# Row maximum norm of an 8192 x 8192 matrix: the SBUF ring and every load at multiples of 512 bytes, and a new list of 33 tail loads

## The chip, the core and the metric

The kernel runs on one core of a Trainium2 chip. The core's engines work side by side, each through its own queue of instructions, and wait for each other on semaphores. Four matter here: the sixteen DMA engines, which copy between HBM (the chip's main memory) and SBUF (the core's working memory of 128 partitions); SP, the queue that issues nearly all of the copies; DVE, the vector engine, which does all of the arithmetic; and Pool, which ends the program. The metric is the device time of one execution in microseconds (us); lower is better. Times come from repeated executions; the profile is one further execution, in which every instruction and every DMA packet is recorded.

## What is computed

```python
def setup_inputs():
    return {"x": np.random.randn(8192, 8192).astype(np.float32)}

def reference(x):
    return np.linalg.norm(x, ord=np.inf, axis=1)
```

For `axis=1` this norm is the largest absolute value of each row. Every one of the 268,435,456 bytes of `x` is read once, and 8192 floats are written.

## The kernel before

The 8192 rows are shared out over 128 partitions, 64 rows to each. Of these, 48 go through the *bulk* and 16 (`n_tail`, the sum of the list `TAIL` over 8192 columns) through the *tail*.

All loads go into one SBUF tile, `ring` (line 229), which holds three slots of 16384 floats in each partition and 256 floats more (`R`, line 214). It is the first tile of the pool. In the built program it begins at byte 16512 of the partition, which is 128 bytes past a multiple of 512; the 128 bytes ahead of it hold four constants of 32 bytes each. The results are collected in `r_bulk` and `r_tail` (lines 230 and 231), behind the ring.

**Bulk** (lines 242 to 250): 24 loads of two rows to each partition. That is 16384 floats, 65536 contiguous bytes, in each of 128 partitions, 8192 KB a load. Load k goes to slot k mod 3. One DVE instruction, `absmax` (lines 233 to 236), reduces it to two maxima. From load 3 on, SP's issue waits until DVE has read what stood in the slot.

**Tail** (lines 253 to 300): in each partition the 16 remaining rows are one run of 131072 contiguous floats, cut into loads whose widths are given by `TAIL`, 31 of them, from 13312 columns down to 576. They are numbered here 24 to 54, after the bulk's 0 to 23. A load can end in the middle of a row, so each load falls into *pieces* of one row each (lines 253 to 261). The piece that ends a row is reduced into `r_tail`. Every other piece is reduced to a partial maximum, which DVE writes into one of the floats of the ring that lie just ahead of the load that will end the row (`slot`, lines 266 to 275). The last piece and its partial maxima are then read in one go: a last piece of 576 columns with nine partial maxima is a read of 585. All in all the tail has 44 reductions.

The place of a load in the ring (lines 270 to 272) is the next multiple of `PAD` = 16 floats, 64 bytes, behind the load before and the room for its partial maxima; where it doesn't fit before the end of the ring, it begins again at the front:

```python
at = -(-(here + n_part) // PAD) * PAD
if at + w > R:
    at = -(-n_part // PAD) * PAD
```

As every width is a multiple of 64 floats, every load reads from a multiple of 256 bytes of `x`. In SBUF six tail loads begin at a multiple of 256 bytes: numbers 26, 29, 34, 37, 38 and 39. All others, the bulk's 24 among them, begin 64, 128 or 192 bytes past one.

**Order.** SP issues the loads in order. An issue waits for DVE where the load overwrites what DVE has to read first, or, as eight semaphores (`DMAHW0` to `DMAHW7`) go round, for the landing of the load eight places before. The order within DVE is that of the loads. The store of `r_bulk` goes out on the queue of ScalarE (ACT) after the last reduction of the third-last load (line 297), and that of `r_tail` on SP after the last reduction (line 301).

Four functions then edit the finished program. `start_first_load_early` puts load 0 ahead of the opening barrier; `drop_implied_waits` takes out waits that another wait covers; `open_without_vector` takes DVE out of the opening barrier; `finish_on_pool` lets Pool alone wait for the last store, after it has cleared the other semaphores. It clears them in one instruction where the last store's semaphore is the first of the range, as here (`DMAHW0`), and otherwise in two, one to each side.

Of the kernel before, what the change touches and what calls it, by code (L numbers as in the profile page):

```python
# [12 lines left out]
F32 = mybir.dt.float32  # L13
X = mybir.AxisListType.X

TAIL = [
    10688, 13312, 11840, 10624, 9472, 8448, 7552, 6720,
    6016, 5376, 4800, 4288, 3904, 3456, 3072, 2688,  # L20
    2432, 2176, 1920, 1728, 1536, 1344, 1280, 1152,
    1024, 896, 832, 704, 640, 576, 576,
]


# [173 lines left out]
@with_exitstack  # L199
def kernel(  # L200
    ctx: ExitStack,
    tc: tile.TileContext,
    x: bass.AP,
    out: bass.AP,
    G: int = 4,
    B: int = 2,
    SLOTS: int = 3,
    PAD: int = 16,
):
    nc = tc.nc  # L210
    P = nc.NUM_PARTITIONS
    rows, cols = x.shape
    W = B * cols
    R = SLOTS * W + PAD * 16


    n_tail = sum(TAIL) // cols
    assert sum(TAIL) == n_tail * cols
    n_bulk_rows = rows // P - n_tail
    assert n_bulk_rows % (G * B) == 0  # L220
    A = n_bulk_rows // (G * B)
    split = n_bulk_rows * P
    x_b = x[:split].rearrange("(a p n b) c -> a n p (b c)", p=P, a=A, n=G, b=B)
    out_b = out[:split].rearrange("(a p n b) -> p a (n b)", p=P, a=A, n=G, b=B)
    x_t = x[split:].rearrange("(p t) c -> p (t c)", p=P)
    out_t = out[split:].rearrange("(p t) -> p t", p=P)

    pool = ctx.enter_context(tc.tile_pool(name="sbuf", bufs=1))
    ring = pool.tile([P, R], F32)
    r_bulk = pool.tile([P, A, G * B], F32)  # L230
    r_tail = pool.tile([P, n_tail], F32)

    def absmax(o, i):
        return nc.vector.reduce_max(  # L234
            out=o, in_=i, axis=X, apply_absolute_value=True
        )

    def after(ins, first, kind):
        info = mybir.DependencyInfo(kind, mybir.DependencyReason.SCHED_ONLY)
        tc.add_manual_dep(ins.ins, first.ins.name, info, reason="order")  # L240

    for a in range(A):
        for n in range(G):
            at = (a * G + n) % SLOTS * W
            t = ring[:, at : at + W]
            nc.sync.dma_start(out=t, in_=x_b[a, n])
            absmax(
                r_bulk[:, a, n * B : (n + 1) * B],
                t.rearrange("p (b c) -> p b c", b=B),
            )  # L250


    pieces, at = [], 0
    for j, w in enumerate(TAIL):
        end = at + w
        while at < end:
            r = at // cols
            to = min(end, (r + 1) * cols)
            pieces.append((j, r, to - at))
            at = to  # L260
    of_row = [[k for k, s in enumerate(pieces) if s[1] == r] for r in range(n_tail)]


    here = A * G % SLOTS * W
    start, slot = [], []
    for j, w in enumerate(TAIL):
        first = next(s for s in pieces if s[0] == j)
        ks = of_row[first[1]]
        n_part = len(ks) - 1 if pieces[ks[-1]][0] == j else 0
# [3 lines that stand above are left out]
        start.append(at)  # L273
        slot.append(at - n_part)
        here = at + w

    src = 0
    for j, w in enumerate(TAIL):
        at = start[j]
        nc.sync.dma_start(out=ring[:, at : at + w], in_=x_t[:, src : src + w])  # L280
        src += w
        here = [k for k, s in enumerate(pieces) if s[0] == j]
        offs = [at + sum(pieces[i][2] for i in here[:m]) for m in range(len(here))]
        todo = list(zip(here, offs))
        if slot[j] != at:

            todo = todo[1:] + todo[:1]
        for k, lo in todo:
            _, r, n = pieces[k]
            ks = of_row[r]  # L290
            if k == ks[-1]:
                frm = slot[j] if len(ks) > 1 else lo
                done = absmax(r_tail[:, r : r + 1], ring[:, frm : lo + n])
            else:
                to = slot[pieces[ks[-1]][0]] + ks.index(k)
                done = absmax(ring[:, to : to + 1], ring[:, lo : lo + n])
        if j == len(TAIL) - 3:

            ins = nc.scalar.dma_start(out=out_b, in_=r_bulk[:])
            after(ins, done, mybir.DependencyClass.Sync)  # L300
    nc.sync.dma_start(out=out_t, in_=r_tail[:])
    nc.at_finalize(drop_implied_waits)
    nc.at_finalize(start_first_load_early)
    nc.at_finalize(finish_on_pool)
    nc.at_finalize(open_without_vector)
# [30 lines left out]
```

## Time and profile before

| What | Value |
|---|---|
| median of 3 runs | 627.94 us (627.76 to 628.19) |
| the profiled execution | 627.77 us, of which 625.1 us are its span |
| bytes moved, mean rate over the span | 268.47 MB, 429 GB/s |
| DVE busy | 553.3 us in 68 reductions (24 bulk, 44 tail) |
| one bulk reduction | 17.22 us |
| one load's issue on SP | 0.33 us |
| last reduction | begins at 623.60 us, takes 0.76 us |
| store of `r_tail` | issued at 624.39 us, lands 1.4 us later |

The span runs from the first instruction to the last; the 2.67 us between it and the time lie around it. The page has a line for each engine's busy time, a row of digits for the share of the DMA engines in 40 equal slices, the DMA queues, and the chain of work that ended last. A load's landing is the moment at which the sixteenth and last increment of its semaphore arrives, one from each DMA engine; the trace keeps the times of all increments, and of every DMA packet its start, duration and size.

### The profile page before, as it was taken

The numbers are of one execution on the slowest core, as the hardware profiler recorded it, in microseconds if no ns is written. First come the engines' busy times: TensorE is split into PE (matmuls) and PEld (weight loads), VectorE is DVE, ScalarE is ACT, GpSimd is POOL, SyncE is SP. The second block draws the span as 40 slices with busy tenths as digits, with TensorE's granted clock in tenths as the row PEclk, the third lists the DMA queues.
The fourth block names the chain that finished last, engine by engine and source line by source line (L and its number), as shares of the span: only waits on it lengthen the run. The fifth ranks groups of instructions, "written<-read, shape, count | busy, mean of one in ns | idle before, by whom it ended". The sixth has DMA issues, their size and how long they took to land.

```text
span 625.1 us, 157 instructions
## 1 busy us (share of the span) xinstructions
DVE 553.3 (89%) x68; POOL 0.2 (0%) x4
## 2 busy tenths in 40 slices
DVE  0588988889988889888898888988889999999999
POOL 0000000000000000000000000000000000000000
DMA  9999999999999999999999999999999999999998
GB/s 403 470 403 457 415 453 419 436 436 415 457 403 470 403 470 403 470 403 457 415 449 424 428 445 403 470 403 470 403 423 450 443 411 441 429 430 423 425 424 333
DMA packets 8705, 268.47 MB, mean 429 GB/s; under 512 B 1664, under 2 KB 1664, under 8 KB 3328
## 3 DMA queue, kind: packets, MB, share of 16 engines
q1 hardware_dynamic: 7920, 268.44, 99.6%
q10 hardware_dynamic: 784, 0.02, 0.1%
q14 instruction: 1, 0.01, 0.0%
HBM read 268.44 MB, written 0.03 MB: 429 GB/s over the span
## 4 chain that ended last, share of the span: by engine, by line
DMA 64%; DVE 35%; another core or an unknown queue 0%; SPq 0%; issue 0%
DMA ring<-in_x_dram 64%; DVE r_bulk L234 25%; DVE ring L234 5%; DVE r_tail L234 5%; SPq L280 0%
## 5 line engine op out<-in xcount | busy, mean ns | idle before, releaser
L234 DVE TENSOR_REDUCE r_bulk<-ring 128x2 f32<-128x16384 f32 x24 | 413.3, 17220 | 70.9 <-DMA ring<-in_x_dram 70.9
L234 DVE TENSOR_REDUCE ring<-ring 128x1 f32<-128x3072 f32 (+25 forms) x28 | 88.8, 3204 | 0.1
L234 DVE TENSOR_REDUCE r_tail<-ring 128x1 f32<-128x8192 f32 (+14 forms) x16 | 53.2, 3330 | 0.1
L320 POOL MEMSET const-bfloat16-1.0<- 128x1 bf16 x1 | 0.1, 102 | 0.0
L320 POOL MEMSET const-uint8-127<- 128x1 uint8 x1 | 0.1, 102 | 0.0
L320 POOL MEMSET const-float32-1.0<- 128x1 f32 x1 | 0.1, 99 | 0.0
L320 POOL MEMSET const-float32-0.0<- 128x1 f32 x1 | 0.1, 98 | 0.2 <-issue 0.2
## 6 DMA issues: line engine op xcount, KB each, us to landing
ring<-in_x_dram SPq DMA_DIRECT2D x1, 6656.0 KB, 30.5
ring<-in_x_dram SPq DMA_DIRECT2D x1, 5920.0 KB, 25.1
ring<-in_x_dram SPq DMA_DIRECT2D x1, 5344.0 KB, 34.1
ring<-in_x_dram SPq DMA_DIRECT2D x1, 5312.0 KB, 37.3
ring<-in_x_dram SPq DMA_DIRECT2D x1, 4736.0 KB, 37.6
ring<-in_x_dram SPq DMA_DIRECT2D x1, 4224.0 KB, 33.5
ring<-in_x_dram SPq DMA_DIRECT2D x1, 3776.0 KB, 30.0
ring<-in_x_dram SPq DMA_DIRECT2D x1, 3360.0 KB, 37.6
```

What stands on the lines that cost most here:

```text
L234: return nc.vector.reduce_max(out=o, in_=i, axis=X, apply_absolute_value=True)
L320: nc = _bacc.Bacc("TRN2", target_bir_lowering=False, num_devices=1)
```

## The change

The ring is allocated last instead of first, behind `r_bulk`, `r_tail` and an unused tile `gap`, whose width brings the ring to a multiple of 512 bytes: in the built program it begins at byte 16896, which is 33 times 512. `PAD` goes from 16 to 128 floats, so every load begins at a multiple of 512 bytes in the partition. The slack behind the three slots goes from 256 to 512 floats. The tail's widths are all multiples of 128 columns, so that every load also reads from a multiple of 512 bytes of `x`; there are 33 loads (24 to 56), from 13440 columns down to 512, instead of 31, and 47 reductions instead of 44. The bulk's loads and reductions are the same in number, size and order.

```diff
+HEAD, STEP = 32, 8
+
 TAIL = [
-    10688, 13312, 11840, 10624, 9472, 8448, 7552, 6720,
-    6016, 5376, 4800, 4288, 3904, 3456, 3072, 2688,
-    2432, 2176, 1920, 1728, 1536, 1344, 1280, 1152,
-    1024, 896, 832, 704, 640, 576, 576,
+    13440, 12800, 11520, 10240, 9088, 8192, 7296, 6528,
+    5760, 5248, 4608, 4096, 3712, 3328, 2944, 2688,
+    2304, 2048, 1920, 1664, 1536, 1408, 1280, 1152,
+    1024, 896, 768, 768, 640, 640, 512, 512,
+    512,
 ]
...
-    PAD: int = 16,
+    PAD: int = 128,
...
-    R = SLOTS * W + PAD * 16
+    R = SLOTS * W + PAD * 4
...
-    ring = pool.tile([P, R], F32)
     r_bulk = pool.tile([P, A, G * B], F32)
     r_tail = pool.tile([P, n_tail], F32)
+    used = [HEAD, A * G * B, n_tail]
+    gap = -sum(-(-n // STEP) * STEP for n in used) % PAD
+    pool.tile([P, gap], F32, name="gap")
+    ring = pool.tile([P, R], F32)
```

Two more loads in the round of eight semaphores move the last store's semaphore from `DMAHW0` to `DMAHW2`, which lies inside the range, so Pool clears in two instructions instead of one.

## The prediction

> **What bounds the kernel now.** I read the page's busy lines first, then the chain of work that ended last, then the timelines of DVE and SP in the tail.
>
> ```profile
> DVE 553.3 (89%) x68; POOL 0.2 (0%) x4
> DMA  9999999999999999999999999999999999999998
> DMA 64%; DVE 35%; another core or an unknown queue 0%; SPq 0%; issue 0%
> L234 DVE TENSOR_REDUCE r_bulk<-ring 128x2 f32<-128x16384 f32 x24 | 413.3, 17220 | 70.9 <-DMA ring<-in_x_dram 70.9
> ```
>
> The DMA engines never rest, and in the bulk DVE is the one that waits: 70.9 us, all of it for loads. The chain, in order of time, gives the pace:
>
> ```profile
> 41.22 17.22 DVE r_bulk L234
> ...
> 466.94 17.22 DVE r_bulk L234
> 484.16 8.59 DVE r_tail L234
> ...
> 608.23 0.02 issue
> 608.25 6.30 DVE ring L234 x4
> ...
> 623.60 0.76 DVE r_tail L234
> ```
>
> Each bulk reduction begins as its load lands: load 1 at 41.22, load 23 at 466.94, so a load lands every 425.72 / 22 = 19.351 us. From 466.94 to the end DVE hardly rests: the tail is 157.4 us of reductions that wait for a landing only here and there, at 608.25 last. So the end hangs on two things: when load 23 lands, and how long DVE's tail takes after it, as long as the loads stay ahead.
>
> **What a start off 256 bytes costs.** In the packet records, packets of 47360 and 10752 bytes (loads 26 and 39, at multiples of 256 bytes) last 1749 and 404 ns: 36608 / 1345 = 27.2 bytes per ns. Each engine carries 8 packets of a load, so a bulk load's bytes alone need 8 x 65536 / 27.2 = 19.275 us; it takes 0.076 more. The tail shows the same excess with both kinds of start side by side. In SP's own timeline each of these issues waits for the landing of the load eight before (36 to 40):
>
> ```profile
> 588.94 0.33 SPq L280 DMA_DIRECT2D ring<-in_x_dram  x1
> 593.02 0.33 SPq L280 DMA_DIRECT2D ring<-in_x_dram  x1
> 596.66 0.33 SPq L280 DMA_DIRECT2D ring<-in_x_dram  x1
> 599.85 0.33 SPq L280 DMA_DIRECT2D ring<-in_x_dram  x1
> 602.78 0.33 SPq L280 DMA_DIRECT2D ring<-in_x_dram  x1
> ```
>
> Loads 37, 38 and 39 took 4.08, 3.64 and 3.19 us; their bytes need 4.066, 3.614 and 3.162. Load 40, which begins 64 bytes off, took 2.93 against 2.861. By the semaphore records, finer than the timeline, the six loads at multiples of 256 land 10, 0, 9, 20, 20 and 27 ns over their bytes, and nearly all others 67 to 90 ns, whether 64, 128 or 192 off.
>
> **Bulk, changed.** All 24 loads now begin at a multiple of 512. The excess of 76 ns can fall to 14 (mean of the six) or 24 (median engine of the last of three such in a row). But another limit stands near: packets on one engine start 2414 ns apart at the closest (1058 gaps in the bulk; two are less), even early, when they run ahead of the landings, and the ninth hand-over, with the semaphore write, adds about 7: 8 x 2414 + 7 = 19.319, an excess of 44. The six aligned loads show 44 to 49 in their packets' ends too; they land faster only because the lag between packet and landing shrinks, from 0.49 to 0.39 us. A lag can't shrink for 24 loads, so I take 44. The gain by load 23 is 23 x (19.351 - 19.319) = 0.73; the other bounds give 23 x 0.052 = 1.20 and 23 x 0.062 = 1.43. No row excludes a loss, but none hints at one; the lower bound is 0.
>
> The Trainium skill, "DMA: Bandwidth & Descriptors", section "How a descriptor splits into AXI transactions", says that a descriptor starting off a multiple of 256 bytes costs a transaction more. The rule asks for 256, so it gives the step from 256 to 512 nothing, and by it alone the whole 8 x 256 / 27.2 = 75 ns would go from each load, an estimate of 1.73 us for the bulk; the packets' spacing says less than half.
>
> **Tail on DVE.** Three reductions more. Durations of 749 ns for 576 columns and 8676 for 8192 give 149 ns fixed, of which 82 overlap the instruction before: 3 x 0.067 = +0.20. Columns are the same. A reduction that waits both for a load and for the partial maximum written just before it starts 34 ns after the one before instead of 82 ns ahead of it; three do so now (593.20, 603.11, 623.60), two will: -0.12. What else keeps DVE waiting in the tail are landings: 26, 13, 61, 208, 24, 49, 26, 10 and 61 ns past the usual overlap, 0.48 in all. If the loads lead, this goes: -0.48. Sum -0.39 (lower bound of the gain: waits stay and +0.08 is left).
>
> **Do the loads lead?** Loads 24 to 54 now land in 623.49 - 466.92 = 156.57 us, 2.37 over their bytes; 0.49 of it is one 8192-byte instruction fetch at 606.7 on one DMA engine (a packet of load 43 lasted 855 ns instead of 265), which the trace shows once in the tail. 33 loads at 0.044, with the fetch, make 1.94, so the last lands at 623.49 - 0.73 - 0.43 = 622.33. DVE's last reduction would end at 624.36 - 0.73 - 0.39 = 623.24, and takes 0.70: it begins at 622.54 and needs the landing 0.11 before. Cover 0.10 us, so DVE decides, just; followed load by load through loads 42 to 47, behind the fetch, the lead is as thin, 0.03 to 0.13. Should the fetch come twice, up to 0.4 of it would show.
>
> The same skill page, "Rules for kernel authors", asks for at least 1 MiB per DMA, which speaks against the new list: 15 loads below that instead of 13. By its table (341 GB/s at 1 MB) the 0.5 MB more in such loads would cost an estimated 0.3 us against the bulk's rate. Here loads of 288 KB land 0.70 to 0.73 us apart, over 400 GB/s.
>
> **Costs that I set at nothing.** SP issues two loads more, 0.33 each; the last is released by a landing seven loads ahead, some 6 us, and a queue is never empty meanwhile (the first packet of a fresh issue comes 1 us later). The store of `r_bulk` leaves after the third-last reduction, about 1.3 us before the last store instead of 1.5, and is down (2.0 us) 0.7 before it (1.4). Pool's extra clear lies in the 0.7 us between the closing barrier and the landing of the last store; Pool's dearest rows are 0.18. Without that cover it costs 0.2 at most. What follows the last reduction, and the 2.67 us around the span, stay.
>
> **Sum.** -0.73 - 0.39 = -1.12 on the profiled 627.77: 626.65. The runs' median is 0.17 above that execution, so 626.8 for the median.
>
> **Rivals.**
> 1. *The packets' spacing falls too.* 2414 may be the price of an unaligned start as well. Then 24 to 14 ns are left: -1.20 or -1.43, and -0.39 in the tail: 626.35 to 626.1. For it: landings came at 14. Against it: the 44 in the aligned loads' packet ends. Chance 0.30.
> 2. *The bulk does not speed up*: the excess belongs to 64 KB packets, not to where they start, and the tail gains at most its waits: 627.94 - 0.39 = 627.55. If starts don't matter at all, so that the change doesn't do what it says, 33 x 0.076 + 0.49 = 3.00 against 2.37 puts the last landing at 624.12 and the end 0.5 later, 628.5. Against it: 76 ns in tail loads of every size off the multiple, and never on it. Chance 0.17.
> 3. *The engines fall into step.* With all starts alike in the 512 bytes, packets of sixteen engines could collide in SBUF as they do when load 0 starts: its packets last 2484 on average, 63 ns over the later 2421, 8 x 63 = 0.50 us a load. In all 24 bulk loads that is +12, near 640. It decides once a bulk load loses 0.10 us ((1.26 + 1.12) / 24). Against it: load 26 begins at a multiple of 512 and took 10 ns over its bytes. Chance 0.05.
>
> **How the numbers follow.** What can be told from no change here is about 0.2%, 1.26 us: below 626.68 is faster, above 629.20 slower. The likeliest case, 0.48, is 626.8, between 626.5 and 627.2 with the fetch and the run-to-run spread; a quarter of it, 0.12, falls on the faster side. Rival 1 is faster (0.30), rival 2 within (0.17), rival 3 slower. So faster 0.42, same 0.53, slower 0.05. The range runs from rival 1's end, 626.0, to the middle of rival 2, 628.0.
>
> **What would show it.** Bulk reductions 19.32 us apart, load 23 landing near 466.2; 19.30 and less is rival 1, 19.35 rival 2. No reduction of the tail waiting for a landing but perhaps one behind the fetch; last reduction ending near 623.2. Packets of 65536 bytes still 2414 ns apart, without the 2418 and 2422 of now. I am wrong if packets start closer than 2414, or if DVE's waits persist because loads of the new tail land later than 0.1 us behind this count.

## The result, and the profile after

| | before | changed |
|---|---|---|
| median | 627.90 us (22 runs) | 626.97 us (22 runs) |
| lowest to highest | 627.72 to 628.33 | 626.61 to 627.65 |
| ratio | | 0.9986, 95% interval 0.9979 to 0.9992 |
| the profiled execution, and its span | 627.77, 625.1 | 627.04, 624.4 |
| load 1's and load 23's reductions begin | 41.22, 466.94 | 41.34, 466.82 |
| from there to the end of the last reduction | 157.42 | 156.83 |

The median fell by 0.93 us, 0.14%: a gain whose interval lies clear of zero, and whose middle lies inside the 0.2% of which the forecast spoke. The forecast was 626.8. The lowest run fell by 1.11 us. In these runs the changed kernel scatters more widely than the kernel before (1.04 us from lowest to highest against 0.61); in the later sets of runs that is not always so.

The page of the changed kernel first (its reductions now stand on line 240):

```profile
DVE 552.8 (89%) x71; POOL 0.2 (0%) x4
...
DMA  9999999999999999999999999999999999999998
...
DMA ring<-in_x_dram 58%; DVE r_bulk L240 25%; DVE ring L240 10%; DVE r_tail L240 6%
...
L240 DVE TENSOR_REDUCE r_bulk<-ring 128x2 f32<-128x16384 f32 x24 | 413.3, 17220 | 70.8 <-DMA ring<-in_x_dram 70.8
```

The picture is the old one: DMA engines never at rest, DVE waiting in the bulk. The change is in the chain of work that ended last, in order of time (start, duration, what):

```profile
41.34 17.22 DVE r_bulk L240
...
234.85 17.23 DVE r_bulk L240
...
408.85 17.23 DVE r_bulk L240
...
466.82 17.22 DVE r_bulk L240
484.04 8.59 DVE r_tail L240
...
592.28 0.02 issue
592.30 6.08 DVE ring L240 x2
...
622.95 0.70 DVE r_tail L240
```

Read it in three steps. From load 1 to load 11 (41.34 to 234.85) a load took 19.351 us, no better than before; from load 11 to load 20 (to 408.85) it took 19.333. Load 23 was 0.12 earlier than before. After it DVE's chain breaks for a landing only once, at 592.30, where before DVE waited in some nine places: 0.59 of the 0.71 us that this execution gained up to the last reduction were gained in the tail.

SP's timeline, with issues that wait for the landings of loads 37 to 40, shows the new pace of the tail:

```profile
592.30 0.33 SPq L286 DMA_DIRECT2D ring<-in_x_dram  x1
595.78 0.33 SPq L286 DMA_DIRECT2D ring<-in_x_dram  x1
598.96 0.33 SPq L286 DMA_DIRECT2D ring<-in_x_dram  x1
601.70 0.33 SPq L286 DMA_DIRECT2D ring<-in_x_dram  x1
```

Loads 38, 39 and 40 took 3.48, 3.18 and 2.74 us; their bytes, at 27.2 per ns, need 3.464, 3.162 and 2.711. How far a load lands *over its bytes* is the time from the landing before to its own, less the time of its bytes at that rate. By the semaphore records the tail loads 25 to 35 land 45 ns over their bytes on average, and 38 to 56 land 36 over.

### The profile page after: what moved, and what is told of

Same layout as the page of the kernel before. It is cut to its first block, busy times and chain, and to the rows that moved or that the text cites. A ratio compares the mean times of both kernels' runs of the same rounds, so it can differ in the third digit from the quotient of the medians.

```text
span 624.4 us, 161 instructions
## 1 busy us (share of the span) xinstructions
DVE 552.8 (89%) x71; POOL 0.2 (0%) x4
## 4 chain that ended last, share of the span: by engine, by line
DMA 58%; DVE 41%; another core or an unknown queue 0%; issue 0%
DMA ring<-in_x_dram 58%; DVE r_bulk L240 25%; DVE ring L240 10%; DVE r_tail L240 6%
## 5 line engine op out<-in xcount | busy, mean ns | idle before, releaser
L240 DVE TENSOR_REDUCE ring<-ring 128x1 f32<-128x512 f32 (+20 forms) x31 | 91.6, 2997 | 0.0
L240 DVE TENSOR_REDUCE r_tail<-ring 128x1 f32<-128x8192 f32 (+12 forms) x16 | 50.2, 3143 | 0.0
## 6 DMA issues: line engine op xcount, KB each, us to landing
ring<-in_x_dram SPq DMA_DIRECT2D x1, 5760.0 KB, 27.2
```

The costliest lines, as they stand in the source:

```text
L240: return nc.vector.reduce_max(out=o, in_=i, axis=X, apply_absolute_value=True)
```

## The experiments

In every kernel here all of the work is done and the arithmetic is the same. "Bulk" is the time from the start of load 1's reduction to that of load 23's; "tail" is from there to the end of the last reduction. Both are of the one profiled execution of each kernel; the medians are of 11 runs (22 in the first two rows).

| kernel | starts in SBUF | tail list | bulk | tail | median | ratio to before (95%) |
|---|---|---|---|---|---|---|
| before | mixed | old | 425.72 | 157.42 | 627.90 | |
| changed | 0 mod 512 | new | 425.48 | 156.83 | 626.97 | 0.9986 (0.9979 to 0.9992) |
| ring alone moved | bulk 0, tail mixed | old | 425.19 | 157.36 | 627.37 | 0.9990 (0.9981 to 0.9999) |
| all 128 off | 128 mod 512 | new | 425.79 | 158.08 | 628.29 | 1.0004 (0.9995 to 1.0013) |
| all at 256 | 256 mod 512 | new | 425.58 | 157.05 | 627.25 | 0.9985 (0.9976 to 0.9993) |
| changed, second | 0 mod 512 | new | 425.16 | 156.84 | 626.75 | 0.9981 (0.9972 to 0.9989) |
| old list, all aligned | 0 mod 512 | old | 425.24 | 157.44 | 627.77 | 0.9995 (0.9986 to 1.0004) |
| tail reads 128 off | 0 mod 512 | new, shifted | 425.89 | 157.02 | 626.99 | 0.9982 (0.9973 to 0.9990) |
| changed, third | 0 mod 512 | new | 425.25 | 156.89 | 626.82 | 0.9980 (0.9971 to 0.9989) |
| before, second | mixed | old | 425.72 | 157.39 | 627.98 | 1.0000 (0.9992 to 1.0009) |
| old list, aligned, second | 0 mod 512 | old | 425.71 | 156.97 | 626.79 | 0.9981 (0.9972 to 0.9990) |
| changed, fourth | 0 mod 512 | new | 425.50 | 157.05 | 626.76 | 0.9983 (0.9974 to 0.9992) |

Rows three to six ran on one chip, and their ratios go against the runs of the kernel before there (median 627.87); the next four ran on a second chip (628.18), the last two on a third (627.90).

**The ring alone.** The kernel before, with the ring allocated last behind 32 unused floats, at byte 16896:

```diff
-    ring = pool.tile([P, R], F32)
     r_bulk = pool.tile([P, A, G * B], F32)
     r_tail = pool.tile([P, n_tail], F32)
+    pool.tile([P, 32], F32, name="gap")
+    ring = pool.tile([P, R], F32)
```

> The kernel before with its ring moved to a multiple of 512 bytes (16896), list and 64-byte steps of the tail as they were: the 24 bulk loads aligned, the tail mixed. Theory A (a start off a multiple of 256 bytes costs each load 75 ns where it lands; without it the packets' spacing of 2414 ns rules, and hiccups of the reading are no longer hidden): packets of 65536 bytes mostly 2414 ns apart, load 23 lands between 466.1 (no hiccup) and 466.8 us instead of 466.92, and the time is 627.2 to 627.8. Theory B (the bulk does not care where it begins; all of the gain is the tail's): spacing 2418 to 2422 as before, load 23 at 466.9, time 627.9.

Its chain of waits:

```profile
466.45 17.22 DVE r_bulk L235
...
623.04 0.76 DVE r_tail L235
```

Load 23 lands 0.49 us earlier (466.45 against 466.94), and 2057 of the gaps between packets in the bulk are 2414 ns, against 1058 before. Loads 16 to 23 land 44 ns over their bytes, against 75. The bulk does care where it begins, and theory B falls. The tail, where 20 loads still begin off a multiple of 256 (25 before), stays as long as it was, 157.36. By the medians (627.37 against 627.87) this is about half of the gain; the interval of its ratio ends at 0.9999, just below 1.

**All loads 128 off.** The changed kernel, its ring 32 floats further on:

```diff
-    pool.tile([P, gap], F32, name="gap")
+    pool.tile([P, gap + 32], F32, name="gap")
```

> The changed kernel with its ring 128 bytes further on: list and steps as changed, every load 128 bytes past a multiple of 512. Theory A: every load lands 76 ns over its bytes, load 23 at 466.9, the tail's last landing 0.5 us later than the kernel before's, time 628.2 to 628.6, slower than before. Theory B: the list alone brings the gain, time about 627.0. If where DVE's reads begin also sets their time, reductions of 640 columns take 816 ns again instead of 807.

The end of its chain, its busiest group on DVE in the tail, and SP's issues that wait for the landings of loads 38 to 40:

```profile
544.82 44.52 DMA ring<-in_x_dram
589.35 0.02 issue
589.37 10.05 DVE ring L240 x3
...
620.74 0.02 issue
620.75 3.68 DVE ring L240 x5
...
624.46 0.70 DVE r_tail L240
```

```profile
L240 DVE TENSOR_REDUCE ring<-ring 128x1 f32<-128x512 f32 (+20 forms) x31 | 92.0, 3003 | 0.6 <-DMA ring<-in_x_dram 0.6
```

```profile
596.86 0.33 SPq L286 DMA_DIRECT2D ring<-in_x_dram  x1
600.10 0.33 SPq L286 DMA_DIRECT2D ring<-in_x_dram  x1
602.88 0.33 SPq L286 DMA_DIRECT2D ring<-in_x_dram  x1
```

The new list with unaligned starts gains nothing: 628.29, where theory A had put it, against 627.87 for the kernel before (the interval of the ratio holds 1). Loads 39 and 40 took 3.24 and 2.78 us, where they took 3.18 and 2.74 in the changed kernel. Bulk loads are 19.354 us apart, tail loads 25 to 35 land 74 ns over their bytes where the changed kernel's land 45 over, and DVE waits for landings again, in the chain the last time at 620.75. Some 1500 of the bulk's gaps are 2414 ns here all the same, against 1839 in the changed kernel: the number of such gaps alone does not tell the pace, the landings do. The same list, instructions and order, moved by 128 bytes, cost 1.5 us against the changed kernel in this pair of medians (628.29 and 626.75). Reductions of 640 columns lasted 809 and 820 ns; in the aligned kernels they lasted 807 to 825, so where DVE's reads begin shows no price.

**All at 256.** The same edit with `gap + 64`.

> The changed kernel with its ring 256 bytes further on: every load begins 256 bytes past a multiple of 512. Theory A: same as the changed kernel, 626.6 to 627.6, spacing 2414. Theory C (it is 512 that counts): spacing above 2414, loads 76 ns over their bytes, time 628.2 to 628.6.

Packets of the bulk start 2414 ns apart in 1956 gaps, loads 16 to 23 land 44 over their bytes and tail loads 25 to 35 land 46 over. Theory C falls: in the landings 512 gives nothing that 256 doesn't. The median, 627.25, is far from theory C's 628.2, but 0.50 above the changed kernel's on the same chip (626.75) and above its other three medians; the lowest run, 626.53, is the lowest of all. In the profiled execution loads 2 to 15 landed late (83 over their bytes on average); whether 256 has a part in that is open.

**The tail's reads 128 off.** The changed kernel, with loads 25 to 56 reading from 128 bytes past a multiple of 256, and still landing at multiples of 512:

```diff
-    13440, 12800, 11520, 10240, 9088, 8192, 7296, 6528,
+    13408, 12800, 11520, 10240, 9088, 8192, 7296, 6528,
...
-    512,
+    544,
```

> The changed kernel with its first tail load 32 columns narrower and its last 32 wider, so that tail loads 25 to 56 read from 128 bytes past a multiple of 256 of x, while all still land at multiples of 512. If the 75 ns belong to where a load lands, nothing happens: tail loads 44 ns over their bytes on average, time 626.6 to 627.6. If a read off 256 costs the same, each of these 32 loads lands 75 or more over its bytes, the tail's last landing is 1.0 us later, and the time 0.6 to 1.0 us over the changed kernel.

Nothing happens: loads 25 to 35 land 44 ns over their bytes, packets of 51200 bytes last 1891 ns in both kernels (1895 where they land 128 off), and the median, 626.99, is 0.17 above the changed kernel's on the same chip, where a price on the reads was to show as 0.6 to 1.0. The 75 ns belong to the side on which a load lands. The Trainium skill ("DMA: Bandwidth & Descriptors", section "How a descriptor splits into AXI transactions") tells of the extra transaction where a descriptor's bytes are fetched; here a read that begins off 256 costs nothing that shows, and a landing does.

This kernel's profiled execution shows something else, in the chain of its bulk:

```profile
60.57 17.23 DVE r_bulk L240
...
118.82 17.23 DVE r_bulk L240
...
177.33 17.23 DVE r_bulk L240
...
235.30 17.23 DVE r_bulk L240
```

From 235.30 back to 177.33 are three loads in 57.97 us, 19.32 each; the six before them took 58.25 and 58.51. Loads 5, 6 and 7 landed 253, 360 and 288 ns over their bytes, the median engine as late as the last. Loads that are late like this are called ragged below. The list of the tail can have no part in this.

**The old list, aligned.** The ring as in the first experiment, and `PAD` 128 with `R = SLOTS * W + PAD * 4`, but the 31 loads of before. It was run twice, each time beside the changed kernel on the same chip (its third and fourth runs).

> The kernel before with the ring at 16896 and PAD 128, so that every load of the OLD list begins at a multiple of 512 in SBUF (its sources stay at multiples of 256 of x). Theory A (starts alone matter): bulk as in the changed kernel (load 23 at 466.4 to 466.8), and in the tail DVE's waits for landings shrink as there; three reductions fewer at 60 ns each. Chain from load 23's landing to the end 156.6 to 157.0 us against 156.83 in the changed kernel and 157.43 before; time 626.6 to 627.5, level with the changed kernel. Theory L (the new list carries the tail's gain): chain near 157.4 as in the run with the ring alone moved, time 627.2 to 627.6.

> The old list with all starts at multiples of 512, a second time, beside the changed kernel on the same chip. In its first profile the chain from load 23's landing to the end was 157.44 us, with DVE waiting 0.40 for the load behind the instruction fetch, 0.18 for a ragged load 29 and 0.35 in three reductions that wait for a load and a partial maximum both. Theory L (the list places these waits): no ragged load this time, but again three such reductions and 0.3 or more behind the fetch, chain 157.1 to 157.4, time 0.3 to 0.6 us over the changed kernel's. Theory A (starts alone): chain 156.8 to 157.0 and the times level within 0.2.

> The changed kernel beside it: chain from load 23's landing to the end 156.83 to 157.05 us, one such reduction (the last) and 0.1 to 0.35 behind the fetch; time 626.6 to 627.6 as its bulk has it.

The first execution pointed to theory L, and the first set of runs, though noisy (626.82 to 628.57), was slower than the changed kernel beside it: 627.77 against 626.82. The second did not bear it out: 626.79 against 626.76, tails of 156.97 and 157.05. In these two executions DVE waits as follows (timelines; first the old list, then the new):

```profile
588.83 4.21 DVE L235 TENSOR_REDUCE ring<-ring 128x1 f32<-128x3904 f32 x1
593.07 3.75 DVE L235 TENSOR_REDUCE r_tail<-ring 128x1 f32<-128x3458 f32 x1
...
602.98 2.69 DVE L235 TENSOR_REDUCE r_tail<-ring 128x1 f32<-128x2434 f32 x1
```

```profile
584.50 3.88 DVE L240 TENSOR_REDUCE r_tail<-ring 128x1 f32<-128x3585 f32 x1
588.61 7.54 DVE L240 TENSOR_REDUCE ring<-ring 128x1 f32<-128x3712 f32 x2 [0.24 <-DMA ring<-in_x_dram]
```

With the old list the reductions at 593.07, 602.98 and the last begin some 35 ns after the one before instead of 82 ns ahead of it, as they did before the change; with the new list only the last does. The new list pays for that with three reductions more. The instruction fetch holds DVE up in both, by 0.32 us past its usual overlap with the new list (at 588.61) and by 0.18 with the old (at 608.09). The two sets of runs differ, 0.95 us for the new list and nothing, so what the list is worth stays open; the second set shows that the gain can be had without it.

**The changed kernel and the kernel before, again.**

> The changed kernel again, for a second profile. Theory A: spacing 2414 with hiccups in other places than in the first profile, and load 23 landing anywhere from 466.1 to 467.0 us with them; the time moves with that landing one for one. Theory B: load 23 at 466.8 again and the spread of the times from elsewhere.

> The changed kernel a third time. Theory A with hiccups: from load 1 to load 23 between 425.02 us (22 x 19.319, none) and 425.6, and the time follows it.

> The kernel before a second time. If its slower landing hides the hiccups of the reading, load 1 to load 23 takes 425.72 us (22 x 19.351) again within 0.1, though single packets are as ragged as in the changed kernel; if the hiccups add up here as well, it scatters by some tenths.

In four profiles of the changed kernel the bulk took 425.48, 425.16, 425.25 and 425.50 us; in two of the kernel before it took 425.72 both times, though only 903 and 1058 of its gaps are 2414 ns. Over all profiles of the table, the three bulks that land off 256 lie between 425.72 and 425.79, the nine that land at multiples of 256 between 425.16 and 425.89: two of these nine gained nothing. What is the same in all is the steady stream behind the ragged loads: loads 16 to 23 land 43 to 47 ns over their bytes in the nine, 75 or 76 in the three.

The time of the changed kernel follows its bulk: of the four, the executions with bulks under 425.3 took 626.79 and 626.82 us, those above 627.04 and 627.29. The fourth also has the 0.24 us behind the fetch. That ragged packets are hidden where the landing is the slower side is what these figures suggest; no run here made packets ragged on purpose, and whether they come from the reading, as the expectations have it, or from elsewhere is open. Nor are the runs of the kernel before as even as its two profiles: they reach from 627.72 to 629.59.

## Why the prediction was right, and where not

1. **What bounds the kernel** held: the landing of load 23, then DVE's tail. In the changed kernel DVE is the last link, as expected, and its last reduction ended at 623.65; 623.24 was foretold.
2. **The mechanism** held. A load that lands off 256 bytes comes 75 ns over its bytes, an aligned one 45; a start at 128 off in every load brought the 75 back, at 256 they were gone, and reads had no part. Packets on one engine stay 2414 ns apart and come no closer (1839 gaps in the changed kernel's bulk; a handful are 2412 or 2413), so the 44 ns of the packets' pace are the new excess: loads 16 to 23 landed 45 over their bytes, and the tail's 25 to 35 as many.
3. **The bulk's gain of 0.73 was mis-sized.** Load 23's reduction began 0.12, 0.40, 0.40 and 0.10 us earlier in the four profiles. Two things were left out. Load 1 came 0.07 to 0.16 later than before, for which I have no cause; aligned starts alone don't explain it, as load 1 came 0.02 to 0.05 later in the other aligned kernels and 0.07 with all loads 128 off. And loads 2 to 15 were ragged: loads 2 to 23 landed 65 over their bytes on average in the first profile and 50 in the best, where I had 44 for all. I had read the fastest spacing as the pace of the whole bulk, and taken the kernel before's steadiness for that of the reading.
4. **The tail's gain of 0.39 was under-sized**: 0.59, 0.58, 0.53 and 0.37. In the kernel before, what DVE lost beyond 60 ns a reduction and 0.96 columns per ns comes to 1.00 us; in the first profile of the changed one it is 0.23. That is 0.78 less, against three reductions at 0.06. I had set the waits' removal at 0.60, measured from the overlap of 82 ns, and three reductions at 0.20, or 0.067 each. Of the reductions that wait for a load and a partial maximum both, one was left (622.95), not two. By that same overlap some 0.54 of the 0.78 are waits; the rest is reductions that lasted a few ns less, which no experiment here explains.
5. **The thin cover** was thin. The fetch came at load 36 or 37 instead of 42 or 43, and DVE was held up there, by 0.11 us past its usual overlap in the first profile and 0.32 in the fourth.
6. **The sum**, -1.12, was too high for the profiled execution (-0.73): its bulk gained 0.61 less than forecast, its tail 0.20 more. The two misses partly cancelled, so that the forecast of 626.8 lies nearer to the medians (626.97 in the result, 626.75 to 626.82 in the repeats) than its terms deserve. The medians' differences are -0.93 in the result, -1.12 and -1.14 on the two chips where the kernel before stood at 627.87 and 627.90, and -1.36 on a third, where its runs reached 629.03. The costs set at nothing held: from the end of the last reduction to the end of the span it is 0.76 us in both kernels.
7. **Rivals.** The packets' spacing did not fall (rival 1), and the bulk did gain (rival 2: the ring alone brought 0.5). The lasting loss of 0.50 us a load of rival 3 did not come: loads 16 to 23 land 43 to 47 over in every aligned kernel. The row that this rival rested on was misread, too: of load 0's eight packets on each engine only the first is long (2933 ns on average, the others 2420), and no run shows a collision in SBUF. Whether the ragged loads are a passing form of one is open. For the rule on loads under 1 MiB, weighed in the forecast, the runs show no price: the new list was level with the old once and faster once.

## What to carry to other kernels

Where DMA engines are the limit and descriptors are long, let every load land at a multiple of 256 bytes in SBUF: here, with 2 to 64 KB a descriptor, that is worth 30 ns a load of 128 descriptors in the steady stream. Moving one tile did it for the bulk, a wider step between the loads for the tail. Price such a gain by the next limit, not by the excess that goes away, and ask what the slower side may have been hiding: two profiles with the same pace to 0.01 us say nothing of how even the stream is once its bottleneck is gone. Before a gain is put down to a re-planned list, run the old list in the new place.

## What the runs showed of the hardware

- A load's landing falls into a cycle once starts are aligned: in the changed kernel's second profile loads 16 to 23 land 27, 5, 43, 91, 36, 5, 34 and 110 ns over their bytes, 44 on average, while packets on each engine keep an even 2414. In the second profile of the kernel before, loads 12 to 23 land an even 66 to 84 over.
- One 8192-byte instruction fetch falls into the tail of every kernel here, at load 42 or 43 with the old list and 36 or 37 with the new, and makes one packet on one DMA engine last 0.47 to 0.65 us longer (855 ns instead of 265 in the kernel before). The load under way lands 0.35 to 0.76 us late by it, and the later loads make up only a part of that.
